# The first layer's MLP by two by two blocks with seven block products, its inner layer kept in DRAM

## The chip, the core and the metric

The kernel runs on one core of a Trainium2 chip. The metric is the device time of one execution in microseconds; the median of the runs shown is compared. The engines are TensorE (PE, with PEld its weight loads), VectorE (DVE), ScalarE (ACT), GpSimd (POOL) and SyncE (SP, which issues most DMAs).

## What is computed

Two layers over 512 latent and 256 context tokens of width 1024, 768 tokens in all. Each layer has three parallel token mixers and then the MLP that the change touches:

```python
def sq_relu_mlp(h, w1, w2):
    return jnp.square(jax.nn.relu(h @ w1)) @ w2

# per layer, D_FF = 4096
hx2 = rmsnorm(x, g_mlp[i]) * (1.0 + sc2x) + sh2x
x = x + g2x * sq_relu_mlp(hx2, w_ff1[i], w_ff2[i])
# in all layers but the last the same for the context tokens
```

All is float32. The last layer needs the latent tokens alone, so the first layer works on 768 tokens and the second on 512.

## The kernel before

Activations lie transposed: a page is a tile of 128 channels by up to 768 tokens, and `pg` hands out 46 such pages. A float32 product is made of three matmuls of a shorter type: each operand is split into a high part, a rounded copy, and a low part, the difference, and `mm_T` (L427 on) issues high by high, high by low and low by high for each of the 8 slices of 128 of the inner dimension. 768 tokens go as segments of 512 and 256 columns.

Weights come as pages of 128 by 1024 numbers (eight 128 by 128 blocks, one output tile) through `Stream`: `load` issues the DMA on SP into one of `NRAW` raw buffers, `split` makes the high part (POOL at L246, or ACT at L244) and `flush` the low part (DVE at L257). `ahead` keeps this one page ahead, with one more load.

The MLP of a layer runs in four chunks c of 1024 inner channels. `ff1(m, sg)` makes one inner tile: 24 matmuls for each segment, relu on ACT (L1661), the square on POOL (L1662), the split on ACT and DVE (L391, L392). Then eight output tiles of the chunk's second product are added to x, scaled by a gate, on DVE (L1686). In the first layer the second product of c = 3 is made in two token groups (`two`, L1700), so that the next layer's norm can begin.

The norm ahead of the MLP runs in two token groups of 384 (`even`). `norm_tail` is a generator: `sum` and `rstd` make the scale per token, `spread` broadcasts it by matmul (L507), and `finish` then scales (L524), shifts (L531) and splits the eight tiles. The second group's tail runs in the background while PE works on the first group's columns of the first five inner tiles (LEAD = 5).

Background generators are advanced by `tick`, once for every 6 matmuls in the MLP; `bg.rate` and `mbg.rate` say how many steps a tick gives. `mods_gen(1)` makes the next layer's modulation in the background at rate 0.3: pairs of multiplications on DVE with accumulation (L371 over 768, L373 over 256 elements, both inputs in SBUF), fed by SP loads into four `ld` buffers. It has 98 steps, of which 66 carry such a pair: 36 of the first 48, and 30 of the last 50.

Each engine takes its instructions in the order in which the program writes them.

Of the kernel before, what the change touches and what calls it, by code (L numbers as in the profile page):

```python
# [21 lines left out]
LAT = 512  # L22
# [15 lines left out]
NRAW = 2  # L38
# [10 lines left out]
def _page_shape(key):  # L49
    kind = key[0]  # L50
    if kind in ("in", "o", "ff1", "ff2", "lru"):
        return 8, 128
    if kind == "tok":
        return key[5], key[3]
    if kind == "qb":
        return key[4], 384
    if kind == "kvb":
        return 2, 512
    if kind == "br":
        return 8, 128  # L60
    raise KeyError(kind)
# [82 lines left out]
def kernel(ctx: ExitStack, tc: tile.TileContext, A: dict, order: list, record: bool, tap=None):  # L144
# [38 lines left out]
    ALT = ("AD", "PD")  # L183
    WOR = 1
# [35 lines left out]
    class Stream:  # L220
# [5 lines left out]
        def load(self, j):  # L226
            while self.nraw <= j and self.nraw < len(order):
                k = order[self.nraw]
                a, b = _page_shape(k)
                t = wp.tile([128, 1024], F32, tag="wr", bufs=NRAW, name=nm("wr"))[:, :a * b]  # L230
                nc.sync.dma_start(t, A["wst"][woff[k]:woff[k] + 128 * a * b].rearrange("(p n) -> p n", p=128))
                self.raw[self.nraw] = t
                self.nraw += 1

        def split(self, j):
            while self.nsp <= j and self.nsp < len(order):
                self.load(self.nsp)
# [22 lines left out]
        def get(self, key):  # L260
            if record:
                order.append(key)
            assert order[self.nget] == key, (order[self.nget], key)
            self.split(self.nget)
            if self.nsp == self.nget + 1:
                self.flush()
            self.nget += 1
            return self.hl.pop(self.nget - 1)

# [43 lines left out]
    rope = cst.tile([128, 2, 4, 32], F32, name="rope")  # L313
# [6 lines left out]
    x_d = drp.tile([8, 128, LAT], F32, name="x_d")  # L320

# [238 lines left out]
    def proj_tok(keys_, hi, lo, toks, N):  # L560
# [24 lines left out]
        return ds_  # L585

# [336 lines left out]
    nc.sync.dma_start(rope, A["rope"])  # L923
# [24 lines left out]
    for i in range(depth):  # L948
# [17 lines left out]
        def small_gen():  # L966
# [3 lines left out]
                                     in1=vc[:, V_MKN:V_MKN + 1], op0=ALU.mult, op1=ALU.mult)  # L970
            for w in range(2):
# [652 lines left out]
        nrm2 = Norm(i, x, V_GMLP, 32, 24, grp)  # L1624
        nf = None
        for g, parts in enumerate(grp):
# [3 lines left out]
            for m in range(8):  # L1630
# [4 lines left out]
                nrm2.stat(m, g, SQ0 if g else None)  # L1635
            if g == 0:
                nf = bg.add(norm_tail(nrm2, 0, *(TL0, TL4)[i]), front=True)
# [6 lines left out]
        mark(f"L{i} mlp")  # L1644
        W.defer = DF[5]
# [176 lines left out]
```

## Time and profile before

| | us |
|---|---|
| median of 3 runs | 2652.65 (2652.08 to 2658.22) |
| the profiled execution | 2651.59 |
| its span, first to last instruction | 2649.8 |
| PE busy | 2486.3 (94%) |
| DVE, POOL, ACT busy | 1614.6, 895.8, 797.6 |
| first layer's MLP, first product to the last chunk's second product | 981.7 to 1470.9 |

The span is what the engines' records cover; the time of the execution lies 1.8 us above it. Rows of a window give the busy time of each engine in it with the count of instructions, the granted clock of PE (1.00 is 2.4 GHz), and the DMA rate. A row of the timeline gives the start, the length, the engine and line, and in brackets the idle time before it and what ended it. Matmul lengths overlap in the pipeline; the spacing of starts is their rate.

### The profile page before, as it was taken

What the parts mean: (1) busy time and instruction counts of PE and PEld (TensorE: products, weight loads), DVE (VectorE), ACT (ScalarE), POOL (GpSimd) and SP (SyncE); (2) the same over time, 40 slices, a digit from 0 to 9 for tenths busy, and PEclk for the clock granted to TensorE, in tenths of its full rate; (3) what the DMA queues carried; (4) which work ended last, traced back from release to release, by engine and by line L of the source; (5) the groups of instructions that cost most, each with busy time, mean ns of one, the idle gap of its engine ahead of it and who ended that gap; (6) DMA issues with size and microseconds to landing.
All of it is one profiled execution on the core that took longest, in us unless ns stands there. A gap on an engine that the chain in (4) does not pass through costs nothing.

```text
span 2649.8 us, 38124 instructions
## 1 busy us (share of the span) xinstructions
PE 2486.3 (94%) x14406; PEld 2194.4 (83%) x14406; DVE 1614.6 (61%) x3303; ACT 797.6 (30%) x1945; POOL 895.8 (34%) x822
## 2 busy tenths in 40 slices
PE   6978999999899998999999989899998898899999
PEld 6868889898788898888888877789887787788887
DVE  7878665775785575655452467565655876643343
ACT  2261241425682122010101125433325741201100
POOL 5232122243342355222222352222253534633222
PEclk6999999999899999999999999999999999899999
DMA  6234322332014433334431322322221045333332
GB/s 222 80 108 157 122 91 88 114 115 83 7 57 167 144 112 110 127 110 145 153 139 61 120 96 80 111 98 78 86 95 55 1 154 166 120 118 95 96 96 96
DMA packets 93255, 282.97 MB, mean 107 GB/s; under 512 B 11152, under 2 KB 11920, under 8 KB 93072
## 3 DMA queue, kind: packets, MB, share of 16 engines
q1 hardware_dynamic: 84240, 257.46, 28.9%
q10 hardware_dynamic: 6912, 15.73, 1.6%
q0 software_dynamic: 1920, 7.34, 0.7%
q8 instruction: 114, 1.87, 0.3%
q14 instruction: 69, 0.57, 0.1%
HBM read 255.33 MB, written 25.17 MB: 106 GB/s over the span
## 4 chain that ended last, share of the span: by engine, by line
PE 65%; DVE 19%; ACT 6%; issue 5%; POOL 4%; DMA 1%; SPq 0%; ACTq 0%; DVEq 0%; POOLq 0%
PE f L438 32%; PE gt L1111 7%; PE S L745 4%; PE pt L576 4%; PE pt L577 4%; PE pt L578 4%; DVE wl L257 3%; PE pv L794 3%; PE T L771 2%; PE br L438 2%; PE wo L438 2%; DVE u L1019 1%; DVE junk L371 1%; ACT junk_a L1408 1%; POOL xn L531 1%
## 5 line engine op out<-in xcount | busy, mean ns | idle before, releaser
L246 POOL TENSOR_SCALAR wh<-wr 128x1024 fp32r<-128x1024 f32 (+2 forms) x297 | 335.9, 1133 | 635.8 <-DMA wr<-wst 244.0
L257 DVE TENSOR_TENSOR wl<-wr,wh 128x1024 fp32r<-128x1024 f32 (+1 forms) x286 | 391.2, 1369 | 151.3 <-POOL wh L246 113.3
L438 PE MATMUL f<-h,wh 128*128 128x512 f32 (+2 forms) x808 | 282.8, 350 | 9.8 <-ACT rl L1661 9.1
L438 PE MATMUL f<-l,wh 128*128 128x512 f32 (+2 forms) x808 | 282.3, 349 | 3.2 <-DVE l L392 3.2
L438 PE MATMUL f<-h,wl 128*128 128x512 f32 (+2 forms) x808 | 280.3, 347 | 0.7 <-DVE wl L257 0.7
L438 PE MATMUL f<-uh,wh 128*128 128x512 f32 (+1 forms) x768 | 273.8, 356 | 5.2 <-DVE x L1700 3.5
L438 PE MATMUL f<-ul,wh 128*128 128x512 f32 (+1 forms) x768 | 273.3, 356 | 0.0
L438 PE MATMUL f<-uh,wl 128*128 128x512 f32 (+1 forms) x768 | 272.1, 354 | 0.0
L631 POOL TENSOR_SCALAR P<-P,rl 128x768 f32<-128x768 f32 (+2 forms) x160 | 136.9, 856 | 384.3 <-DVE rl L630 274.8
L1111 PE MATMUL gt<-h,wh 128*128 128x512 f32 (+1 forms) x576 | 220.0, 382 | 6.8 <-POOL wh L246 5.9
L392 DVE TENSOR_TENSOR ul<-rl,uh 128x768 fp32r<-128x768 f32 (+3 forms) x74 | 66.6, 899 | 255.0 <-ACT uh L391 255.0
L577 PE MATMUL pt<-wl,h 128*128 128x256 f32 (+2 forms) x720 | 211.4, 294 | 10.0 <-DVE wl L257 10.0
L1661 ACT ACTIVATE rl<-f 128x768 f32<-128x768 f32 (+3 forms) x74 | 46.7, 632 | 573.7 <-PE f L438 573.7
L576 PE MATMUL pt<-wh,h 128*128 128x256 f32 (+2 forms) x720 | 214.1, 297 | 5.4 <-POOL wh L246 3.3
L1111 PE MATMUL gt<-h,wl 128*128 128x512 f32 (+1 forms) x576 | 207.7, 361 | 8.8 <-DVE wl L257 8.8
L578 PE MATMUL pt<-wh,l 128*128 128x256 f32 (+2 forms) x720 | 211.0, 293 | 0.0
L1111 PE MATMUL gt<-l,wh 128*128 128x512 f32 (+1 forms) x576 | 208.1, 361 | 0.0
L1662 POOL TENSOR_TENSOR rl<-rl 128x768 f32<-128x768 f32 (+3 forms) x74 | 85.8, 1159 | 315.2 <-ACT rl L1661 315.2
L402 DVE TENSOR_TENSOR ptl<-T,pth 128x384 fp32r<-128x384 f32 (+2 forms) x288 | 132.2, 490 | 97.8 <-ACT pth L396 96.3
L438 PEld LDWEIGHTS f<-h,wh 128*128 128x128 f32 x808 | 155.0, 192 | 29.7 <-issue 5.6
L438 PEld LDWEIGHTS f<-l,wh 128*128 128x128 f32 x808 | 154.8, 192 | 21.5 <-DVE l L392 4.4
L438 PEld LDWEIGHTS f<-h,wl 128*128 128x128 f32 x808 | 154.3, 191 | 18.7 <-DVE wl L257 1.1
(279 smaller groups left out, 6235.3 us busy)
## 6 DMA issues: line engine op xcount, KB each, us to landing
wr<-wst SPq DMA_DIRECT2D x298, 512.0 KB, 3.5
mod<-wmod SPq DMA_DIRECT2D x108, 384.0 KB, 4.3
bias<-bias SPq DMA_DIRECT2D x32, 320.0 KB, 3.6
th_d<-th ACTq DMA_DIRECT2D x24, 384.0 KB, 2.4
thr<-th_d SPq DMA_DIRECT2D x24, 384.0 KB, 3.5
x<-x SPq DMA_DIRECT2D x16, 384.0 KB, 4.9
th_d<-th ACTq DMA_DIRECT2D x24, 256.0 KB, 2.0
thr<-th_d SPq DMA_DIRECT2D x24, 256.0 KB, 3.8
```

The source lines that it names most:

```text
L246: pool.tensor_scalar(hi, t, 1.0, 0.0, op0=ALU.mult, op1=ALU.add)
L257: eng.tensor_tensor(out=lo, in0=t, in1=hi, op=ALU.subtract)
L402: dve.tensor_tensor(out=lo, in0=ps, in1=hi, op=ALU.subtract)
L438: pe.matmul(ps[:, c:c + b - a], wt[:, k, :], mv[k][:, a:b], start=k == 0 and wt is wh and mv is hi, stop=k == kts - 1 and wt is wl)
L576: pe.matmul(o, hi[kk][:, c], wh[:, k, :], start=kk == 0, stop=False)
L577: pe.matmul(o, hi[kk][:, c], wl[:, k, :], start=False, stop=False)
L578: pe.matmul(o, lo[kk][:, c], wh[:, k, :], start=False, stop=kk == total - 1)
L631: pool.tensor_scalar(self.P[:, :w], self.P[:, :w], rl, 1.0, op0=ALU.mult, op1=ALU.mult)
L745: pe.matmul(S[:, c:c + ww], a[r0:r1, qc], b[r0:r1, k0:k0 + ww], start=i_ == 0, stop=i_ == 2)
L794: pe.matmul(o[:, a:b], v_block(V, t, h), mv, start=i_ == 0, stop=i_ == len(ops) - 1, skip_group_check=True)
L1111: pe.matmul(ps[:, :b - a], wt[:, k, :], mv[k][:, a:b], start=k == 0 and wt is wh and mv is hi, stop=k == KT - 1 and wt is wl)
L1662: pool.tensor_tensor(out=t[:, a:b], in0=t[:, a:b], in1=t[:, a:b], op=ALU.mult)
```

## The change

In the first layer (`BLK = (True, False)`) the two products of the MLP are computed by blocks. Output channels are taken in pairs of tiles (m and m + 4), the inner dimension of a product in two halves of 512, and tokens in two halves of 384 columns, which gives 2 by 2 by 2 blocks. A Strassen-Winograd scheme forms a pair's four output blocks from seven block products (12 matmuls of 384 columns each) in place of eight. There are 16 pairs for the first product and 12 for chunks 0 to 2 of the second; chunk 3 stays as it was.

- **Weights**: `BlockWeights` holds two raw pages of a pair; POOL makes four sums of 128 by 512 from them, in place where it can, and ACT and DVE split each of the seven operands. Splits are five products ahead. `NRAW` becomes 3 for the whole kernel, and the `rope` table moves from its own buffer into a loaded page in each layer.
- **Activations**: `block_tail` replaces `norm_tail`; for the second token group it also forms sums of blocks and splits seven operands for each of 4 slices.
- **Inner layer**: all 16 pairs of the first product run first. The squared blocks and their sums are stored to DRAM (`u_d`) by ACT's queue, loaded again by SP six products ahead of use, and split by ACT and POOL three products ahead.
- **Order**: `seq` lists (pair, product). The first five pairs have products 1 and 2 made ahead on the first token group. Ticks come twice for each product, and `mods_gen(1)` starts at product 39.

```diff
-NRAW = 2
+NRAW = 3
+    BLK = (True, False)
+    BLEAD = (5, 5)
+    BAHEAD = 5
+    BLOAD, BSPLIT = 6, 3
+    TB0 = 6, 8, 4, "DPDPDPDP"
+    TB1 = 5, 4, 1, "DPDPDPDP"
+    u_d = [drp.tile([16, 3, 128, TOK], F32, name=f"u_d{i}") for i in range(depth)]
...
+    BLOCKS = {1: ("w11", "11"), 2: ("w12", "21"), 3: ("s4", "22"), 4: ("w22", "4"), 5: ("s1", "1"), 6: ("s2", "2"), 7: ("s3", "3")}
...
+        def sums(self, j):
+            if j < len(self.seq) and self.seq[j][1] == 6:
+                p = self.seq[j][0]
+                w11, w21, w22 = self.half(p, 0, 0), self.half(p, 1, 0), self.half(p, 1, 1)
+                pool.tensor_tensor(out=w11, in0=w11, in1=w21, op=ALU.subtract)
+                s2 = self.f[p, "s2"] = pg("s2")[:, :512]
+                pool.tensor_tensor(out=s2, in0=w22, in1=w11, op=ALU.subtract)
+                pool.tensor_tensor(out=w21, in0=w21, in1=w22, op=ALU.add)
+        def split(self, j):
...
+            if q == 6:
+                s4 = self.f[p, "s4"] = pg("s4")[:, :512]
+                pool.tensor_tensor(out=s4, in0=self.half(p, 0, 1), in1=src, op=ALU.subtract)
+            t = self.t[p, name] = wp.tile([128, 1024], F32R, tag="wh", bufs=8, name=nm(name))
+            split_block(t, 512, src)
...
+    def split_block(t, n, src, eng=dve):
+        act.activation(t[:, :n], src, AF.Copy)
+        eng.tensor_tensor(out=t[:, n:2 * n], in0=src, in1=t[:, :n], op=ALU.subtract)
...
+                for eng, o, p, q in ((pool, b3, b22, b12), (dve, b12, b12, b11), (dve, b2, b22, b12), (pool, b21, b21, b2)):
+                    eng.tensor_tensor(out=o, in0=p, in1=q, op=ALU.subtract)
+                yield
+                for j, (name, src, eng) in enumerate((("2", b2, dve), ("1", b12, dve), ("3", b3, pool), ("4", b21, pool), ("22", b22, dve))):
+                    O[name][kk] = pg("h" + name, F32R)
+                    split_block(O[name][kk], n, src, eng)
...
+        for k in range(KT) if g == 0 else (0, 4, 1, 5, 2, 6, 3, 7):
...
+            for p in range(BLEAD[i]):
+                seq += [(p, 1), (p - 1, 2)] if p else [(p, 1)]
+            seq.append((BLEAD[i] - 1, 2))
+            for p in pairs:
+                for q in (6, 5, 7, 3, 4) if p < BLEAD[i] else (1, 3, 6, 5, 7, 2, 4):
...
+            dmul = lambda t: pool.tensor_tensor(out=t, in0=t, in1=t, op=ALU.mult)
...
+            def add(out, ps, t):
+                dve.tensor_tensor(out=out, in0=ps[:, :n], in1=t, op=ALU.add)
...
+                        act.dma_start(u_d[i][p, slot][:, :2 * n], S[p][k][:, :2 * n])
...
+                    def sums():
+                        Z = st["Z"] = pg("bz")
+                        for o, a, b in ((Z[:, h1], Y[:, h1], Y[:, h0]), (Y[:, h0], Y[:, h0], X[:, h0]), (Z[:, h0], Y[:, h1], Y[:, h0])):
+                            pool.tensor_tensor(out=o, in0=a, in1=b, op=ALU.subtract)
+                    if last or p < 12:
+                        later(j + 1, sums)
+                    later(j + 4, lambda: store(p))
...
+            def xadd(m, h, src):
+                for s, a, b in grp[h]:
+                    dve.scalar_tensor_tensor(out=x[m][:, a:b], in0=src[:, a - h * n:b - h * n], scalar=mods[i][:, s, 40 + m:41 + m],
+                                             in1=x[m][:, a:b], op0=ALU.mult, op1=ALU.add)
...
+                if j == nlead:
+                    bg.finish(nf)
+                    bg.rate = 0.5
+                if not last and j == nlead + 5 * BLEAD[i] + 4:
+                    spread_c()
+                    mgen = mbg.add(mods_gen(i + 1))
+                    mbg.rate = 0.3
+                BW.ahead(j + BAHEAD)
...
+                for o, name in splits.get(j, ()):
+                    vs = uf.pop((o, name))
+                    if name == "4":
+                        for k in range(4):
+                            pool.tensor_tensor(out=vs[k], in0=vs[k], in1=vs[4 + k], op=ALU.subtract)
+                    for k in range(4):
+                        O[o][name][k] = pg("u" + name, F32R)
+                        split_block(O[o][name][k], n, vs[k], pool)
...
+                for k in range(4):
+                    for i_, (w0, b0) in enumerate(((0, 0), (0, n), (512, 0))):
+                        pe.matmul(ps, wt[:, w0 + 128 * k:w0 + 128 * k + 128], B[k][:, b0:b0 + n],
+                                  start=fresh and k == 0 and i_ == 0, stop=k == 3 and i_ == 2, skip_group_check=True)
+                    if k % 2:
+                        tick()
```

Between the last of `seq` and chunk 3, eight stored tiles are loaded whole, split on ACT and in turn on DVE and POOL (`plain_load`, `plain_split`), and the weight stream `W` starts again.

## Rows read from the trace of the kernel before

**Rows 1.** The page: busy time by engine, and the chain that ended last.

```profile
PE 2486.3 (94%) x14406; PEld 2194.4 (83%) x14406; DVE 1614.6 (61%) x3303; ACT 797.6 (30%) x1945; POOL 895.8 (34%) x822
...
PE 65%; DVE 19%; ACT 6%; issue 5%; POOL 4%; DMA 1%; SPq 0%; ACTq 0%; DVEq 0%; POOLq 0%
```

**Rows 2.** Windows: length, then busy (count) of PE, PEld, DVE, ACT, POOL; clock, DMA.

```profile
0.00:100.00 100.00, 78.10 (x402) 69.75 (x403) 74.39 (x174) 26.42 (x35) 48.00 (x33) 0.78 0.51 184
981.60:1024.00 42.40, 32.22 (x169) 29.78 (x169) 26.52 (x44) 11.97 (x25) 31.48 (x34) 0.96 0.19 69
1076.30:1470.70 394.40, 394.40 (x2256) 346.10 (x2255) 189.48 (x394) 38.16 (x46) 85.49 (x69) 1.00 0.34 121
981.60:1470.70 489.10, 478.92 (x2735) 424.03 (x2735) 245.83 (x486) 61.76 (x90) 137.15 (x119) 1.00 0.34 119
```

**Rows 3.** Timeline of PE: starts twelve matmuls apart, 512 and 256 mixed, then 384.

```profile
1080.27 0.40 PE L438 MATMUL f<-uh,wh 128*128 128x512 f32 x1
...
1082.37 0.40 PE L438 MATMUL f<-uh,wh 128*128 128x512 f32 x1
```

**Rows 4.** The same of the 384-column matmuls of the lead.

```profile
990.50 0.33 PE L438 MATMUL f<-h,wl 128*128 128x384 f32 x1
...
992.58 0.33 PE L438 MATMUL f<-h,wl 128*128 128x384 f32 x1
```

**Rows 5.** Timeline of PE around the lead's end: rows with idle time before them.

```profile
996.10 0.91 PE L507 MATMUL R<-sq,ones_f 128*128 128x384 f32 x2 [1.63 <-POOL sq L497]
...
1014.34 0.66 PE L438 MATMUL f<-h,wh 128*128 128x384 f32 x1 [5.34 <-ACT rl L1661]
...
1022.50 0.44 PE L438 MATMUL f<-h,wl 128*128 128x384 f32 x1 [0.74 <-DVE wl L257]
```

**Rows 6.** Timeline of DVE and POOL, four instructions that meet.

```profile
962.41 1.23 DVE L257 TENSOR_TENSOR wl<-wr,wh 128x1024 fp32r<-128x1024 f32 x1 [1.60 <-ACT wh L244]
962.49 2.03 POOL L524 TENSOR_TENSOR xn<-x,sq 128x384 f32<-128x384 f32 x1
963.55 1.37 DVE L392 TENSOR_TENSOR l<-xn,h 128x384 fp32r<-128x384 f32 x1
964.63 1.23 POOL L531 TENSOR_SCALAR xn<-xn,G,mods 128x384 f32<-128x384 f32 x1
```

**Rows 7.** Single lines around the first layer's MLP: count, shortest, median, longest (ns).

```profile
L392 DVE TENSOR_TENSOR l<-xn,h x16: 544/546/1385, 963.6 to 1020.1; 128x384 fp32r<-128x384 f32 x16
...
L371 DVE SCALAR_TENSOR_TENSOR junk<-mod,sB x58: 947/951/1803, 1080.6 to 1379.7; 128x768 bf16<-128x768 f32 x58
...
L373 DVE SCALAR_TENSOR_TENSOR junk<-mod,sB x59: 424/425/1140, 1079.5 to 1380.7; 128x256 bf16<-128x256 f32 x59
...
L1633 DVE SCALAR_TENSOR_TENSOR x<-wo,g1h,x x24: 336/469/618, 916.9 to 987.2; 128x384 f32<-128x384 f32 x8, 128x128 f32<-128x128 f32 x8, 128x256 f32<-128x256 f32 x8
...
L477 POOL TENSOR_TENSOR sq<-sq,sq x6: 1009/1016/1024, 926.1 to 983.1; 128x384 f32<-128x384 f32 x6
...
L1662 POOL TENSOR_TENSOR rl<-rl x7: 822/829/1207, 988.7 to 1028.7; 128x384 f32<-128x384 f32 x7
...
L531 POOL TENSOR_SCALAR xn<-xn,G,mods x16: 449/558/2132, 998.8 to 1017.0; 128x128 f32<-128x128 f32 x8, 128x256 f32<-128x256 f32 x8
```

**Rows 8.** Groups by line and shape: count, then busy us and mean ns.

```profile
L257 POOL TENSOR_TENSOR wl<-wr,wh 128x384 fp32r<-128x384 f32 x4 | 4.1, 1028 | 0.3
...
L477 POOL TENSOR_TENSOR sq<-sq,sq 128x512 f32<-128x512 f32 x3 | 3.9, 1308 | 0.1
...
L392 DVE TENSOR_TENSOR ul<-rl,uh 128x768 fp32r<-128x768 f32 x26 | 24.9, 958 | 126.7 <-ACT uh L391 126.7
...
L391 ACT ACTIVATE uh<-rl 128x384 fp32r<-128x384 f32 x10 | 5.3, 525 | 21.4 <-POOL rl L1662 21.4
```

**Rows 9.** DMA: rate by slices of 10 us from 1076, and the weight loads.

```profile
GB/s 136 133 131 101 143 127 52 172 93 54 172 143 54 219 124 183 168 96 216 156 110 153 155 133 131 171 110 247 132 185 52 52 54 52 55 64 95 53 55 52
...
wr<-wst SPq DMA_DIRECT2D x298, 512.0 KB, 3.5
```

More of the change, by code (lines that the diff above doesn't have):

```diff
@@ L268, in get, with bar @@
             return self.hl.pop(self.nget - 1)
+        def bar(self):
+            self.flush()
+            if record:
+                order.append(BAR)
+            assert order[self.nget] == BAR and self.nsp == self.nraw == self.nget
+            self.nget = self.nsp = self.nraw = self.nget + 1
         def ahead(self):
@@ L970, in small_gen @@
                                      in1=vc[:, V_MKN:V_MKN + 1], op0=ALU.mult, op1=ALU.mult)
+            rope = ld("rope")[:, :256].rearrange("p (a b n) -> p a b n", a=2, n=32)
+            nc.sync.dma_start(rope, A["rope"])
+            yield
             for w in range(2):
@@ L1624, with bkeys @@
         nrm2 = Norm(i, x, V_GMLP, 32, 24, grp)
+        if BLK[i]:
+            n = nq // 2
+            pairs = list(range(16 + 4 * (4 if last else 3)))
+            oset = lambda p: 0 if p < 16 else 1 + (p - 16) // 4
+            O = [{name: [None] * 4 for name in U_AT} for _ in range(5)]
+            hf = {}
+            def bkeys(p):
+                if p < 16:
+                    m = 8 * (p // 4) + p % 4
+                    return ("ff1", i, m), ("ff1", i, m + 4)
+                c, m = divmod(p - 16, 4)
+                return ("ff2", i, c, m), ("ff2", i, c, m + 4)
+            seq, prev = [], None
+            for p in range(BLEAD[i]):
[3 more added lines that the diff above has]
+                for q in (6, 5, 7, 3, 4) if p < BLEAD[i] else (1, 3, 6, 5, 7, 2, 4):
+                    if q != 3:
+                        seq.append((p, q))
+                    elif prev is not None:
+                        seq.append((prev, 3))
+                prev = p
+            seq.append((prev, 3))
         nf = None
@@ L1635 @@
                 nrm2.stat(m, g, SQ0 if g else None)
+                if BLK[i] and g and m >= 6:
+                    if m == 6:
+                        BW = BlockWeights(seq, [bkeys(p) for p in range(len(pairs))])
+                        BW.load()
+                    else:
+                        W.bar()
+                        BW.ahead(1)
             if g == 0:
-                nf = bg.add(norm_tail(nrm2, 0, *(TL0, TL4)[i]), front=True)
+                nf = bg.add(block_tail(nrm2, 0, O[0], hf, n, *TB0) if BLK[i] else norm_tail(nrm2, 0, *(TL0, TL4)[i]), front=True)
         bg.finish(nf)
```

261 lines of the change are left out of this document (259 added, 2 removed).

## The prediction

> **What bounds the kernel now.** I read the page first, then windows over the first layer's MLP, then single lines. TensorE is busy 94% of the span and the chain is PE for 65% [rows 1]. In the MLP the bound is plainer: from 1076.3 to 1470.7 PE is busy all 394.4 us at full clock, while DVE has 189.5, POOL 85.5 and ACT 38.2 us of work [rows 2]. Every matmul removed there is worth its spacing, as long as the other engines keep up. So two things must be priced: the matmuls, and the work on DVE and POOL that is added for them.
>
> **Spacing.** Twelve matmuls, half of 512 and half of 256 columns, take 2.10 us [rows 3]; twelve of 384 columns take 2.08 us [rows 4]. The same columns cost the same, 0.175 and 0.1733 us a matmul.
>
> **What DVE and POOL do to each other.** Four instructions meet [rows 6]. DVE starts a weight subtraction at 962.41 and ends at 963.64. POOL's product starts at 962.49, 1.02 us long when alone (as at L477) [rows 7], takes 2.03 and ends at 964.51, 0.88 after DVE's end. DVE's next subtraction, 0.55 us when alone [rows 7], starts at 963.55, takes 1.37 and ends at 964.92, 0.41 after POOL's end. POOL's next one again waits for that. They take turns, and only about 0.13 us of each POOL and 0.14 us of each DVE instruction lies under the other's. It holds for DVE instructions with both inputs in SBUF: those with an input in PSUM never exceed 0.618 us in 24 (L1633) [rows 7]. Before the change this costs little: 189.5 + 85.5 us, not all of it on this path, in 394.4 us [rows 2].
>
> The Trainium skill, page "SBUF — State Buffer", section "Who interferes with whom", speaks against this change: a VectorE instruction with two SBUF inputs and a GpSimd instruction that reads SBUF exclude each other, and the later one waits until the first has finished. Read strictly, whole instructions would add up; the rows agree on the turns but let 0.13 to 0.14 us overlap, and the measurement decides. What the strict rule gives is the rival "whole instructions" below.
>
> **Prices on this shared path** (duration alone less the overlap). POOL with two inputs, 384 columns: 1.016 [rows 7], the very split operation 1.028 [rows 8], so 0.88; 512 columns 1.308 [rows 8], so 1.18; a square in place 0.829 [rows 7], so 0.70; a shift of a tile in two pieces 0.449 + 0.558 [rows 7], so 0.75. DVE split of 384: 0.41. Of 512 no row stands; between 0.546 for 384 [rows 7] and 0.958 for 768 [rows 8] I take 0.68 by the line, so 0.54. A modulation pair 0.951 + 0.425 [rows 7], so 1.10. An addition into x from SBUF 0.47 for 384 columns, 0.53 for 128 and 256 (0.618, 0.336, 0.469 [rows 7], less the overlap).
>
> **The change, part by part.**
>
> *Matmuls.* Before, 28 pairs x 96: 2448 at 0.175 and the lead's 240 at 0.1733, 470.0 us. After, 28 x 84 = 2352 at 0.1733, 407.7 us. Removed: 62.3 us. A pair now takes PE 14.56 us, a second pass of a lead pair (five products) 10.4.
>
> *A later pair of the first product.* POOL: four weight sums 4.72, four squares 2.80, three sums of blocks 2.64. DVE: seven splits 3.78. Path 13.9 us, under PE's 14.56: pair 5 runs at PE's speed. From pair 6 modulation runs too: 14 ticks x 0.3 = 4.2 steps, 0.75 of them with a pair, 3.45 us: path 17.4 us, six pairs 104.3. Pairs 12 to 15 form no sums of blocks: 14.75, together 59.0.
>
> *The lead pairs' second pass.* POOL 4.72 + three squares 2.10 + 2.64, DVE five splits 2.70: 12.2 us against PE's 10.4; five 60.8.
>
> *A pair of the second product.* POOL 4.72; DVE splits 3.78, modulation 4.2 x 0.6 x 1.10 = 2.76, additions into x from SBUF 1.53: 12.8 us, under PE. But for every group of four pairs the stored blocks come back: 28 splits and 4 differences, all on POOL, 28.2 us, in one pair's time. Four pairs have 51.2 + 28.2 = 79.4 us on the path and 58.2 on PE: 19.8 a pair, 238 for twelve.
>
> *The hand-over after the lead.* The five first passes end on PE near 1009: 981.7 + 20.8 + some 6 us of waits for the norm, which stay. The tail can begin only when the scale is spread, 997 [rows 5]. What it and its neighbours then put on the path: POOL four scales 3.5, eight shifts 6.0, eight block differences 7.0, eight splits 7.0, weight sums 3.5, squares 2.5; DVE four scales, eight differences and twelve splits 9.8, weights 3.8; 43.1 in all, less 2.6 that stand behind the first product's last operand. So that product ends near 1038.5 in place of 1010.5: PE waits 28 us. Before it waited 6.8 there, in four places of which the longest and the last stand in [rows 5].
>
> *Given back:* weights are split five products ahead, about 8 us of path work that need not be done in time. *Chunk 3's start:* POOL four subtractions of 768 (twice a 384, 1.8 each), DVE four and the stream's own splits, some 16 us of path in the last six products, 12.5 us of PE: 3 us.
>
> *Sum.* 20.8 + 28 + 60.8 + 14.6 + 104.3 + 59.0 + 238 - 8 + 3 = 520.5 us, against 470.0 + 6.8 = 476.8: 43.7 longer.
>
> *Edits with small prices.* The third raw buffer lets every page's load start a page earlier in the whole kernel: DMA is 1% of the chain [rows 1], so the gain lies between 0 and 26 us; 5 taken, since the MLP, its largest user, has no such wait. ACT: some nineteen copies of about 0.53 [rows 8] for a pair, 10 of 14.6 us, hidden. Its 48 stores stand behind POOL's last sum, and weight copies queue behind them; that delay is POOL's, already counted, and the data are read at least four pairs later. On SP the 32 loads of a group wait for pages, and modulation and weight loads queue behind them: 6.3 MB at the best slice's 247 GB/s [rows 9] are 25 us, under a 40 us stretch of path; 0 taken, up to 9 a group if POOL were faster. The rope load hides under the layer's first projections; uncovered, about the 3.5 of a weight load [rows 9], twice. The clock: in 981.6:1024 PE had 32.2 of 42.4 us and 0.96; in the first 100 us, 78% busy, 0.78 [rows 2]. If the lead's wait brought 0.78 over such a stretch, 7 us; 0 taken.
>
> **Forecast.** 2651.59 + 43.7 - 5 = 2690 us. The profiled execution lies 1.06 us under the median, which changes nothing here.
>
> **Rivals.**
>
> *POOL alone* (faster). If DVE always gives way without being late itself, POOL's own durations decide: PE waits 21 at the hand-over, the lead pairs take 10.8 each, plain pairs follow PE, and a returning group needs 32.5 on POOL plus 8.9 of weight sums in 25 us of PE plus some 8 of running ahead, 8.5 late three times. 20.8 + 21 + 54.1 + 160.2 + 174.7 + 25.5 + 3 = 459.3, 17.5 less: with the buffer's 5, 2629. For it: the blocks are listed ahead, and queues run ahead of PE. Against: DVE itself was held up [rows 6].
>
> *DMA behind it* (no change). The same, with 9 us of loads in each group: 2656.
>
> *PE alone* (faster). All is hidden: 407.7 + 6.8 against 476.8, 62.3 less, 2584 with the buffer. Against: POOL's 32.5 us in a pair's time.
>
> *Whole instructions* (slower still). By full durations: hand-over 38, lead pairs 14.2, pair 5 16.4, pairs 6 to 11 20.7, 12 to 15 17.7, second product 23.9: 20.8 + 38 + 71 + 16.4 + 124.2 + 70.8 + 286.8 - 8 + 3 = 623, 146 longer, 2792. It would also stand in for a clock that falls in the waits.
>
> *Eight products after all:* 2688 matmuls would stay; the diff's `seq` has seven to a pair, so only the count of rows can refute it; no chance given.
>
> **How the numbers follow.** Forecast 0.50, by itself 2660 to 2735; whole instructions or part of the way there 0.14; POOL alone 0.20; PE alone 0.06; DMA behind it, or gain and loss that cancel, 0.10. Slower by over 0.3% (8 us, about what a measurement of this kernel can tell from no change): 0.50 + 0.14 = 0.64. Faster: 0.20 + 0.06 and 0.01 of the cancelling case, 0.27. Within: 0.09. The range leaves out PE alone, the better edge of POOL alone and the worse half of whole instructions: 2622 to 2755.
>
> **What would show it.** 2352 matmuls of 384 columns in the blocks, 0.173 us apart where PE does not wait. PE idle about 28 us after the ten first products, ended by a `split_block` line on DVE or ACT behind POOL. Three stretches in the second product, one where each group returns, each with POOL busy nearly throughout and PE waiting 15 to 25 us for a split of stored blocks. POOL's two-input rows of 384 with a mean well over 1.02 and DVE's splits of 512 over 0.68. PE busy in pairs 6 to 11 at about 84%. Wrong it is if POOL and DVE together exceed the length of a stretch and PE still does not wait: then the turns cost less than [rows 6] say.

## The result and the profile after

The changed kernel takes 2851.53 us (median of four, 2850.63 to 2853.6) against 2652.36 us before in the same session: a ratio of 1.0749, 95% interval 1.073 to 1.0767. The forecast was 2690 with a range up to 2755. The direction was right, the loss five times too small: +199 us where +38 were expected.

The page of after, busy time and chain, which answer to [rows 1]:

```profile
PE 2505.5 (88%) x14070; PEld 2233.4 (78%) x14070; DVE 1816.0 (64%) x3533; ACT 959.5 (34%) x2308; POOL 1167.5 (41%) x1055
...
PE 54%; DVE 19%; POOL 10%; issue 8%; ACT 6%; DMA 3%; SPq 0%; ACTq 0%; POOLq 0%; DVEq 0%
```

PE's share of the chain falls from 65 to 54%, though fewer matmuls run. POOL's rises from 4 to 10, "issue" from 5 to 8 and DMA from 1 to 3.

**Where it went.** By PE's first and last block matmul the block stretch runs from 987.5 to 1653.2; the same work took 981.7 to 1470.9 before. That is 665.8 against 489.2 us, 176.6 longer. The rest lies outside it: 7.5 in the output projection ahead of it, 2.6 at chunk 3, 12.4 in the second layer up to its MLP and 3.5 in that, less 1.7 at the beginning: 200.9 in all, and the spans differ by 200.8.

Windows of after by stage: length, then busy (count) of PE, PEld, DVE, ACT, POOL; clock, DMA. In order: first and second pass of the lead pairs, pair 5, pairs 6 to 11, pairs 12 to 15, the three chunks of the second product, and all of them:

```profile
987.50:1027.20 39.70, 25.82 (x135) 24.28 (x136) 20.81 (x35) 13.31 (x28) 21.03 (x20) 0.89 0.22 76
1027.20:1136.40 109.20, 62.88 (x302) 58.39 (x301) 46.56 (x65) 27.85 (x54) 71.70 (x69) 0.78 0.20 73
1136.40:1163.60 27.20, 20.95 (x117) 20.44 (x117) 10.70 (x13) 10.06 (x20) 17.38 (x16) 0.87 0.41 155
1163.60:1289.40 125.80, 102.43 (x506) 98.71 (x505) 89.73 (x147) 40.35 (x82) 77.95 (x65) 0.89 0.40 148
1289.40:1368.70 79.30, 65.95 (x338) 62.26 (x337) 54.45 (x95) 28.18 (x59) 47.33 (x39) 0.94 0.45 161
1368.70:1464.60 95.90, 71.04 (x339) 64.90 (x338) 66.33 (x116) 38.34 (x81) 64.10 (x53) 0.84 0.49 178
1464.60:1563.20 98.60, 70.22 (x338) 63.36 (x337) 68.87 (x110) 34.74 (x71) 65.01 (x51) 0.88 0.46 163
1563.20:1653.20 90.00, 69.50 (x337) 64.88 (x338) 77.93 (x118) 29.81 (x56) 59.43 (x45) 0.85 0.55 192
...
987.50:1653.20 665.70, 488.81 (x2399) 457.23 (x2400) 435.36 (x693) 222.64 (x450) 423.92 (x352) 0.86 0.40 146
```

Against [rows 2] DVE's work in the MLP grew from 245.8 to 435.4 us and POOL's from 137.2 to 423.9. But no engine is full here: POOL is busy 64% of the stretch, DVE 65%, ACT 33%. And the clock, 1.00 before, is 0.78 to 0.94.

**Floor, clock, waits.** The distance from each of the 2352 block matmuls to the next sorts itself: 0.173 us (the floor of [rows 4]), some 0.32 us, or a wait of over 0.4. What the second class has above 0.1733 us stands under "clock", what the third has above it under "waits":

| stage | length | floor | clock | waits | waits forecast |
|---|---|---|---|---|---|
| lead pairs, both passes | 148.9 | 72.8 | 7.4 | 68.3 | 36.8 |
| pair 5 | 27.2 | 14.6 | 0.5 | 12.1 | 0 |
| pairs 6 to 11 | 125.8 | 87.4 | 12.2 | 25.8 | 16.9 |
| pairs 12 to 15 | 79.3 | 58.2 | 5.2 | 15.5 | 0.8 |
| second product | 284.5 | 174.7 | 23.0 | 85.9 | 63.3 - 8 |
| all | 665.8 | 407.7 | 48.3 | 207.6 | 109.8 |

The forecast column is the prediction's stage sums less the floor. The floor came out as forecast. The waits are nearly twice as long, 98 us more. Of the 48 us under "clock" some 41 are matmuls at the lower clock, which had been taken as 0; the other 7 are the first distance behind a wait, 0.28 us at full clock.

**How a wait is made.** A timeline of after, one pair of the first product (rows of other engines left out):

```profile
1208.24 0.55 DVE L1851 TENSOR_TENSOR by<-fc,by 128x384 f32<-128x384 f32 x1
1208.82 0.52 ACT L1847 ACTIVATE by<-by 128x384 f32<-128x384 f32 x1 [3.52 <-DVE by L1851]
...
1209.42 0.83 POOL L1842 TENSOR_TENSOR by<-by 128x384 f32<-128x384 f32 x1 [4.95 <-ACT by L1847]
...
1210.33 1.34 POOL L1901 TENSOR_TENSOR bz<-by 128x384 f32<-128x384 f32 x1
...
1211.75 1.34 POOL L1901 TENSOR_TENSOR by<-by,bx 128x384 f32<-128x384 f32 x1
...
1213.17 1.61 POOL L1901 TENSOR_TENSOR bz<-by 128x384 f32<-128x384 f32 x1
...
1214.74 1.44 POOL L648 TENSOR_TENSOR wr<-wr,wr 128x512 f32<-128x512 f32 x1
1216.26 1.26 POOL L650 TENSOR_TENSOR s<-wr,wr 128x512 f32<-128x512 f32 x1
...
1217.55 0.63 ACT L681 ACTIVATE s<-s 128x512 fp32r<-128x512 f32 x1 [6.79 <-POOL s L650]
1218.09 0.47 ACT L1884 ACTIVATE by<-fb 128x384 f32<-128x384 f32 x1
...
1218.61 6.00 PE L2011 MATMUL fb<-h,w 128*128 128x384 f32 x24 [3.88 <-ACT by L1884]
```

DVE adds, ACT applies relu, POOL squares, forms three sums of blocks and the next pair's weight sums; ACT then copies such a sum. That copy is needed five products later, yet it stands in ACT's queue ahead of the evacuation L1884, for whose bank PE waits. The round trip is 10.4 us, 1208.24 to 1218.61. POOL has work in it from 1209.42 almost to the end, but POOL, too, had waited 4.95 us for ACT. Each engine waits in turn.

The waits of after over pair 6 to the end of the blocks, us in total, times, longest:

```profile
ACT s L681 <- POOL s L650: 98.5, 18, 13.5
DVE s L682 <- ACT s L681: 90.0, 38, 14.3
ACT by L1847 <- DVE by L1851: 60.1, 21, 4.2
ACT u L681 <- POOL uf L1987: 52.9, 12, 18.2
POOL wr L648 <- DVE w L682: 50.2, 9, 18.4
POOL by L1842 <- ACT by L1847: 50.1, 13, 4.9
PE fb L2011 <- ACT by L1925: 41.9, 8, 9.5
...
PE fb L2011 <- ACT by L1884: 25.6, 10, 3.9
```

Read as a ring: ACT for POOL, POOL for DVE and ACT, DVE for ACT, ACT for DVE. PE's own longest entries name ACT's evacuations L1925 and L1884, which have nothing to do with POOL except their place in the queue.

**The clock.** Windows of after across that wait:

```profile
1208.00:1212.00 4.00, 4.00 (x24) 3.79 (x24) 2.82 (x5) 1.95 (x4) 2.42 (x3) 1.00 0.88 330
1212.00:1216.00 4.00, 2.73 (x16) 2.41 (x14) 3.04 (x5) 0.00 (x0) 3.92 (x3) 1.00 0.00 0
1216.00:1220.00 4.00, 1.39 (x6) 1.39 (x7) 1.79 (x2) 1.01 (x2) 3.92 (x4) 0.93 0.41 160
1220.00:1224.00 4.00, 4.00 (x17) 4.00 (x17) 2.85 (x6) 1.05 (x2) 1.25 (x2) 0.64 0.36 139
```

PE runs 24 matmuls in 4 us at 1.00, waits 3.88 us, and is then busy all 4 us for only 17, at a granted clock of 0.64, part of it at the lower of its two levels (1.2 GHz). This follows the wait in pair after pair: 351 of the 2352 matmuls lie 0.26 to 0.40 us behind the one before, 0.320 in the median. 286 of them fall where the granted clock is at that lower level; the other 65 stand right behind a wait, at full clock. Such a stretch counts as busy PE: of the 102.43 us in pairs 6 to 11 (fourth of the stage windows above) only 87.4 are matmuls at full rate.

### The profile page after: what moved, and what is told of

Its sections match the earlier page's. It is cut to its first block, busy times and chain, and to the rows that moved or that the text cites. A ratio compares the mean times of both kernels' runs of the same rounds, so it can differ in the third digit from the quotient of the medians.

```text
span 2850.6 us, 38722 instructions
## 1 busy us (share of the span) xinstructions
PE 2505.5 (88%) x14070; PEld 2233.4 (78%) x14070; DVE 1816.0 (64%) x3533; ACT 959.5 (34%) x2308; POOL 1167.5 (41%) x1055
## 4 chain that ended last, share of the span: by engine, by line
PE 54%; DVE 19%; POOL 10%; issue 8%; ACT 6%; DMA 3%; SPq 0%; ACTq 0%; POOLq 0%; DVEq 0%
PE f L457 13%; PE gt L1259 8%; PE S L891 4%; PE pt L595 4%; PE pt L596 4%; PE pt L597 4%; PE br L457 3%; PE pv L940 3%; DVE wl L268 2%; PE T L917 2%; PE lu L457 2%; DVE junk L390 2%; PE fb L2011 2%; PE wo L457 2%; POOL u L682 1%
## 5 line engine op out<-in xcount | busy, mean ns | idle before, releaser
L390 DVE SCALAR_TENSOR_TENSOR junk<-mod,sB 128x768 bf16<-128x768 f32 x132 | 156.9, 1189 | 22.4 <-DMA mod<-wmod 21.7
L415 ACT ACTIVATE pth<-T 128x384 fp32r<-128x384 f32 (+2 forms) x288 | 115.3, 440 | 152.5 <-PE T L917 148.0
L596 PEld LDWEIGHTS pt<-wl,h 128*128 128x128 f32 x720 | 139.6, 194 | 11.8 <-DVE wl L268 11.7
L457 PE MATMUL f<-uh,wh 128*128 128x512 f32 (+1 forms) x384 | 143.8, 375 | 4.8 <-DVE x L2039 4.8
L457 PE MATMUL f<-uh,wl 128*128 128x512 f32 (+1 forms) x384 | 143.2, 373 | 0.0
L457 PE MATMUL f<-ul,wh 128*128 128x512 f32 (+1 forms) x384 | 143.2, 373 | 0.0
L595 PEld LDWEIGHTS pt<-wh,h 128*128 128x128 f32 x720 | 139.3, 193 | 4.9 <-POOL wh L257 1.8
L597 PEld LDWEIGHTS pt<-wh,l 128*128 128x128 f32 x720 | 139.5, 194 | 0.0
L1259 PEld LDWEIGHTS gt<-h,wl 128*128 128x128 f32 x576 | 111.3, 193 | 34.8 <-DVE wl L268 18.0
L1259 PEld LDWEIGHTS gt<-h,wh 128*128 128x128 f32 x576 | 111.8, 194 | 29.7 <-POOL wh L257 6.1
L2011 PE MATMUL fb<-h,w 128*128 128x384 f32 x444 | 97.7, 382 | 42.5 <-ACT by L1884 25.6
```

The lines of the kernel that those rows point to most:

```text
L390: dve.scalar_tensor_tensor(out=junk, in0=t, scalar=1.0, in1=sB[s], op0=ALU.mult, op1=ALU.mult, accum_out=acc[:, s, j, 0:1])
L415: act.activation(hi, ps, AF.Copy)
L457: pe.matmul(ps[:, c:c + b - a], wt[:, k, :], mv[k][:, a:b], start=k == 0 and wt is wh and mv is hi, stop=k == kts - 1 and wt is wl)
L595: pe.matmul(o, hi[kk][:, c], wh[:, k, :], start=kk == 0, stop=False)
L596: pe.matmul(o, hi[kk][:, c], wl[:, k, :], start=False, stop=False)
L597: pe.matmul(o, lo[kk][:, c], wh[:, k, :], start=False, stop=kk == total - 1)
```

## The experiments

Times are medians of four executions or more; the runs with free weights, with free sums, with short modulation pairs, without POOL's pair work and with two constant writes have a single one each. Four executions of one kernel lie up to 8 us apart, so an effect of under 5 us says little.

**The third raw buffer alone, and the rope table alone.** `BLK` off leaves the prior MLP with three raw buffers and the moved table; with `NRAW = 2` besides, the table alone.

```diff
-    BLK = (True, False)
+    BLK = (False, False)
```

> The block scheme switched off in both layers, so that only the third raw weight buffer and the moved rope load remain of the change. The prediction took 5 us off for them. Up to the output projection of the first layer the changed kernel ran 1.7 us ahead of the one before, but its second layer took 16 us more. If the buffer or the rope load caused that, this kernel takes 2660 to 2668 us; if the second layer's loss comes from what the blocks leave behind, 2645 to 2652.

> Block scheme off and two raw weight buffers as before: only the rope load's new place is left of the change. With three buffers the same kernel was 0.39% slower than the one before. If the third buffer costs that, this one takes 2650 to 2656; if the rope load does, about 2664.

Measured 2664.44 (ratio 1.0039, 1.0024 to 1.0054) and 2653.5 (1.0005, 0.9996 to 1.0015). The table costs nothing; the third buffer costs some 10 us where 5 were counted as a gain. From the second layer's first product to its output projection 681.8 us stand against 673.5 before. There PE's wait for a weight split has grown (waits of PE in the second layer, of before and of the run with the buffer):

```profile
PE gt L1111 <- DVE wl L257: 2.6, 2, 1.6
```

```profile
PE gt L1259 <- DVE wl L268: 7.5, 2, 7.3
```

Why an earlier load should delay that split was not followed further.

**Nothing waits for the weight sums; nothing waits for any sum.** POOL makes the same three weight sums into a page that no one reads, and the splits read raw halves; then the stored blocks' differences go the same way. The operands are not the scheme's.

```diff
-                pool.tensor_tensor(out=w11, in0=w11, in1=w21, op=ALU.subtract)
+                pool.tensor_tensor(out=s2, in0=w11, in1=w21, op=ALU.subtract)
...
-pool.tensor_tensor(out=vs[k], in0=vs[k], in1=vs[4 + k], op=ALU.subtract)
+pool.tensor_tensor(out=vs[4 + k], in0=vs[k], in1=vs[4 + k], op=ALU.subtract)
```

> POOL makes the same four weight sums of 128 by 512 for each pair, but three of them into a scratch page, and the splits of those operands read the raw weights: the block products use wrong weights, the work on every engine stays. Theory of order: ACT and DVE carry the evacuations of the products just made behind weight copies that wait for POOL's sums; without that wait PE's waits for evacuations shrink, 60 to 110 us less, 2740 to 2790. Theory of the shared path: POOL and DVE still take the same turns, so no more than 10 us less, 2840 or above.

> As the kernel with free weights, and the four differences of stored blocks go to the page that is not split, so that ACT's copies do not wait for POOL there either (the products use wrong operands there). ACT waited 53 us for these differences. Theory of order: 20 to 40 us less than with free weights alone, near 2725, and the block stretch, 665.8 us in the changed kernel, comes near the 533 of the prediction's sum of turns. Theory of the shared path alone: no change.

2827.54 and 2818.84: 24 and 33 us back, where the theory of order had expected 60 to 110 and 20 to 40 more, and that of the shared path 10 at most. Both missed, and the second step, 9 us between two single executions, is hardly clear of noise. The edit takes more away than ACT's waits: as the sums no longer overwrite the raw halves, POOL's own wait for DVE's splits (L648, 50.2 us in the list above) goes too. In pairs 6 to 11 ACT's wait for POOL's sums, 38.8 us in after, was gone, but its relu's wait for DVE's add grew, here in after and with free sums:

```profile
ACT by L1847 <- DVE by L1851: 31.0, 12, 4.2
```

```profile
ACT by L1847 <- DVE by L1851: 49.6, 12, 7.4
```

The wait had changed hands, half of it.

**Sums of blocks behind the next pair's weight sums**, order alone:

```diff
-                        later(j + 1, sums)
+                        after_w.setdefault(j + 2, []).append(sums)
```

> Only an order is changed: POOL's three sums of squared blocks, some 3.7 us for a pair, stand behind the weight sums of the next pair instead of ahead of them; the work and the result are the same. Theory of order: the weight copies on ACT are released some 3 us earlier in each of the twelve pairs, and with them the evacuations: 20 to 40 us less, 2810 to 2830. Theory of the shared path: no change, within 5 us of 2851.

2846.59 (1.0721, 1.0703 to 1.0738): 5 us. The theory of order missed here; which of POOL's sums comes first matters little.

**Short modulation pairs.** DVE's multiplications for layer 1's modulation take 32 columns; layer 2 gets wrong modulations.

```diff
-                dve.scalar_tensor_tensor(out=junk, in0=t, scalar=1.0, in1=sB[s], op0=ALU.mult, op1=ALU.mult,
+                dve.scalar_tensor_tensor(out=junk[:, :nb], in0=t[:, :nb], scalar=1.0, in1=sB[s][:, :nb], op0=ALU.mult, op1=ALU.mult,
```

> The modulation pairs of the second layer work on 32 columns in place of 768 and 256 (the second layer then runs on wrong modulations); their number, steps and loads stay. The prediction charged the shared path 3.45 us of them for each of ten pairs of the first product and 2.76 for each of twelve of the second, 67.6 us. Theory of the shared path (turns set the time): 60 to 75 us less, about 2783. Theory of order (the engines wait on one another in program order, not for lack of time): under 30 us less, 2820 or above.

2793.78: 58 us back, near the 68 charged and well above the 30 that the theory of order allowed. This run shortens DVE's own queue and the turns at once, so it does not tell the two apart.

**POOL's pair work left out**: no weight sums, no sums of blocks, no low parts of stored blocks, squares on 32 columns.

> POOL's part of the block pairs is left out, apart from squares of 32 columns: no weight sums, no sums of squared blocks, no differences and low parts of stored blocks (PE reads the high part twice there). Loads, stores, ACT, DVE and PE keep their work. Both theories expect most of the loss back: with PE's pace in all pairs and only the hand-over of the tail left, the block stretch takes about 455 of the 666 us, 2640 in all. If more than 2700 remains, DVE and ACT alone, without POOL, hold PE up, and POOL is not the cause.

2688.53: 163 back, and still 36 above before; some 2640 had been expected. So most of the loss needs POOL's work, and a part does not. The lead's passes take 113.9 us against a floor of 72.8: the hand-over costs 41 by itself.

**Constant writes in place of POOL's sums**: two, then three whole ones, then three narrower ones that add up to about the sum's lone length. POOL reads nothing from SBUF there; only in the norm tail and at chunk 3 it still does, in 34 us of work. A write waits for whatever holds the place it writes, but no longer for an operand that was only read.

```diff
+    def fill(t):
+        m = t.shape[-1]
+        c = {384: 294, 512: 408}[m]
+        for a in (0, m - c, 0):
+            pool.memset(t[:, a:a + c], 0.01)
-                pool.tensor_tensor(out=w11, in0=w11, in1=w21, op=ALU.subtract)
+                fill(w11)
```

> Each two-input POOL instruction of the block pairs becomes two writes of a constant over the same columns: POOL stays busy for a similar time and every wait stays, but it reads no SBUF (the block operands are wrong). If such writes do not take turns with DVE, DVE's splits of 512 columns fall back to about 0.68 us. Theory of the shared path: POOL's own durations are then all that counts, and the time is that of the rival POOL alone, near 2660 to 2690. Theory of order: POOL's bursts still hold ACT's copies and with them the evacuations, so no more than 60 us less, 2790 or above. It depends on how long the writes take: POOL's busy time in the stretch has to stay near the 380 us of the changed kernel.

> As the run with two constant writes in place of each two-input POOL instruction of the block pairs, but with three: POOL reads nothing from SBUF there and keeps every wait, and its own work is now longer than the sums were when alone (3 x 0.418 = 1.25 us for 384 columns against 1.02, 3 x 0.526 = 1.58 for 512 against 1.31). If the turns on the shared path made the loss, DVE's splits of 512 stay at 0.69 us and most of the 122 us stays given back: 2740 to 2785. If it was the length of POOL's own queue that made it, POOL's longer work brings the time to after's or beyond: 2840 to 2900.

> As the runs with two and three constant writes in place of each two-input POOL instruction of the block pairs, but three narrower writes (294 of 384 columns, 408 of 512), sized from the rows 0.418 and 0.526 so that together they take about what the sum took alone: 1.02 and 1.31 us. POOL then reads nothing, holds DVE up nowhere, keeps its waits and has the length it would have without any turns. If the turns with DVE are the loss and POOL's own length is not, it stays with the two-write run (2729): 2725 to 2750, and the rest up to 2851.5 is what the turns cost. If POOL's own length in a chain of hand-overs is the loss, it lies on the line between two writes (POOL busy 320 us in the stretch, 2729) and three (465 us, 2836): at about 390 us 2780 (2765 to 2800), and the turns cost the 70 that are left.

2729.18, 2835.98 (1.0688, 1.0672 to 1.0704) and 2789.7 (1.0511, 1.0495 to 1.0527). Windows over the block stretch of the three runs, in this order, columns as above:

```profile
987.10:1529.80 542.70, 449.78 (x2399) 433.49 (x2400) 315.01 (x689) 223.29 (x450) 305.34 (x667) 0.92 0.50 177
```

```profile
988.00:1632.00 644.00, 483.33 (x2399) 445.59 (x2400) 316.09 (x689) 222.91 (x450) 448.85 (x983) 0.87 0.42 150
```

```profile
991.80:1589.00 597.20, 467.17 (x2399) 440.48 (x2400) 315.64 (x689) 223.17 (x450) 374.29 (x983) 0.89 0.45 161
```

DVE's 315 to 316 us are the same in all three, so the writes do not hold it up; only POOL's length differs: 305, 374, 449 us give stretches of 543, 597, 644. Each microsecond on POOL costs 0.6 to 0.8 us, although POOL is idle 30 to 44% of the time. Near its lone length (597.2) next to nothing shares a path, and the stretch is 189 us over the floor. What the turns add is 665.7 - 597.2 = 68.5 us of the stretch; in time, 2851.5 - 2789.7 = 62. That is their least, since the squares, too, became three writes, each of 0.345 us (a group of the last run):

```profile
L683 POOL MEMSET by<- 128x294 f32 x84 | 29.0, 345 | 46.7 <-ACT by L1856 43.5
```

Three of them are 1.04 us, and a square alone takes 0.83 [rows 7]: 13 us too much for 64 squares, at the price above an estimated 8 to 11 us of the stretch.

The first of the three runs by itself looks like proof of the turns (122 us back). It is not: two writes are also 20% shorter than the sum (0.84 for 1.02, 1.05 for 1.31), and the third run showed what that is worth. The second, 16 us under after, looks like proof against them, because its POOL has more than its lone work.

That DVE is held up by turns, on the other hand, is plain from the splits of 512 columns, here in after and in the last run (groups by shape: count, busy us, mean ns, idle before):

```profile
L682 DVE TENSOR_TENSOR w<-wr,w 128x512 fp32r<-128x512 f32 x65 | 52.3, 815 | 15.1 <-ACT w L681 14.0 <-DMA mod<-wmod 1.1
L682 DVE TENSOR_TENSOR s<-s,s 128x512 fp32r<-128x512 f32 x43 | 49.4, 1148 | 68.0 <-ACT s L681 67.6
...
L682 POOL TENSOR_TENSOR u<-uf,u 128x384 fp32r<-128x384 f32 x84 | 104.7, 1283 | 0.1
```

```profile
L689 DVE TENSOR_TENSOR w<-wr,w 128x512 fp32r<-128x512 f32 x65 | 44.2, 687 | 20.0 <-ACT w L687 18.8 <-DMA mod<-wmod 1.1
...
L689 DVE TENSOR_TENSOR s<-s,s 128x512 fp32r<-128x512 f32 x43 | 29.7, 690 | 96.6 <-ACT s L687 55.0 <-POOL u L683 41.5
```

815 and 1148 ns fall to 687 and 690; the estimate of 0.68 was right.

**Squares on ACT.**

```diff
-            dmul = lambda t: pool.tensor_tensor(out=t, in0=t, in1=t, op=ALU.mult)
+            dmul = lambda t: act.activation(t, t, AF.Square)
```

> The squares of the inner blocks go from POOL (both inputs in SBUF) to ACT's square function; nothing else changes. Turns on the shared path: four squares a pair of 0.70 to 0.83 us leave it, three for a lead pair, so pairs 6 to 11 fall from 21.0 to about 18, pairs 12 to 15 from 19.8 to about 17, pair 5 by 3, the lead pairs' second pass by 10 to 12: together some 45 us, 2806 (2795 to 2820). ACT has 45.6 of 125.8 us of work in pairs 6 to 11 and takes four times about 0.5 more. Order of ACT's queue (the squares stand ahead of evacuations there): a gain of 15 at most, or a loss: 2836 to 2865.

2848.07 (1.0733, 1.0717 to 1.0749), 3 us, which is within the noise, where the theory of turns had expected 45. Pairs 6 to 11 of that run, columns as above:

```profile
1161.50:1287.00 125.50, 101.15 (x505) 97.00 (x505) 86.83 (x143) 50.73 (x102) 57.71 (x42) 0.90 0.40 148
```

POOL has 20 us less, ACT 10 more, the length is the same. The square has only moved to another engine of the same ring; a bound by the sum of DVE's and POOL's work is refuted here.

**Splits behind the evacuation**, order alone: POOL's sums stay, ACT's and DVE's splits are issued after the product's evacuation. Each copy then also has one product (2.1 us) more behind its sum.

```diff
-                BW.ahead(j + BAHEAD)
+                BW.sums(j + BAHEAD + 1)
...
                 (evac1 if p < 16 else evac2)(j, p, q)
+                BW.ahead(j + BAHEAD)
```

> Order alone, all work kept: POOL's weight sums and the differences of stored blocks stay where they are, but ACT's and DVE's splits of weights and of stored blocks stand behind the evacuation of the product, not ahead of it; so an evacuation no longer stands behind a copy that waits for POOL, and a copy has one product (2.1 us) more behind its sum. Order theory (an in-order queue passes POOL's lateness on to PE): ACT's wait for POOL's sums falls from 6.5 us a pair to about 4, some 2 us for each of 28 pairs, and the waits of 18 us for returned blocks shrink: 2795 to 2825. Throughput of the shared path: the same work, within 10 us of 2851: 2841 to 2856.

2813.99 (1.0602, 1.0586 to 1.0618): 37 us back with all work kept. Pairs 6 to 11 fall from 125.8 to 110.2 us. Two waits of that run from 1130 to 1620, which is the part of after's list and 20 us of pair 5:

```profile
ACT s L682 <- POOL s L651: 55.5, 16, 5.7
ACT u L682 <- POOL uf L1992: 51.8, 12, 16.2
```

98.5 has become 55.5 (51.2 from pair 6 on). What reaches PE is told by the waits of PE that end at one of ACT's evacuations: over all blocks they were 97 us in after, 25.6 of them at L1884, and are 64 here, none of them at that line. So 32 of the 37 us are found where the theory of order has them. The returned blocks' wait (52.9) stays, and chunks 0 to 2 with it: 280.0 against 284.5 us.

**Both of ACT's waits away**: the free sums and the short pairs in one.

> Two earlier edits in one: ACT's copies wait for none of POOL's weight sums and stored-block differences (these still run, into pages that nothing reads), and the layer-1 modulation pairs on DVE take 32 columns. Left out: the seven weight operands are not the scheme's, and layer 2 gets wrong modulations. Alone they gave 33 and 58 us. If ACT's waits for POOL and DVE's lateness are separate losses, they add: 2760 (2750 to 2770). If they are two ways into one loop (ACT waits for whichever of the two is later), taking away both gives more than the sum, as each alone only hands the wait to the other: 2720 to 2750. If one loss was counted twice, less: 2775 to 2795.

2766.83 (1.0421, 1.0404 to 1.0439): 85 back, 33 + 58 less 6. The two losses add; they are not one counted twice.

**Norm tail five steps earlier; the order edits joined; weights seven products ahead.**

```diff
-    TB1 = 5, 4, 1, "DPDPDPDP"
+    TB1 = 0, 4, 1, "DPDPDPDP"
...
-    BAHEAD = 5
+    BAHEAD = 7
```

> The second token group's norm tail begins five background steps earlier (its sum of squares stands some 8 us earlier in PE's order). My hand-over term took the scale as spread 15.3 us after the first product; it is spread 16.9 after it, and the start itself is 5.8 later. If the chain of scale, shift, differences and splits sets the hand-over from that start, the lead's two stretches (148.9 us together) fall by 6 to 9 us: 2843. If the hand-over is set by what stands ahead of the chain in POOL's and DVE's queues (weight sums and weight splits), by less than 3: 2849 to 2852.

> Three changes of order together, all work kept: splits behind the evacuation, POOL's sums of squared blocks behind the next pair's weight sums, the second norm tail five steps earlier. Alone they gave 37, 5 and 0 us. If each removes waits of its own: 2809 (2800 to 2815). If the second and third matter only once ACT no longer stands in front (the wait had only changed hands): 2780 to 2800. If they cancel the first's room: 2816 to 2830.

> As the joined order, with weights made ready seven products ahead in place of five: sums and copies both two products (4.2 us) earlier. If what is left of ACT's wait for POOL's sums (5.7 us at the longest) is lateness that two products can cover, 15 to 30 us below the joined order. If POOL comes to these sums late because of what stands ahead of them in its own queue for the same pair, the head start is no cover: within 8 us of the joined order.

2851.79 (1.0746, 1.073 to 1.0762), 2811.72 (1.0598, 1.0582 to 1.0614) and 2805.66 (1.0573, 1.0555 to 1.0591). The second is the sum of its parts, and the two products' head start of the third gives 6 us more, as was expected if POOL comes to its sums late by what stands ahead of them in its queue. In the first, the lead's passes fell from 148.9 to 145.5 us, but the median did not move; as a small term of the whole it is not settled. Squares on ACT, sums behind the weight sums and the earlier tail in one kernel gave 2843.85 (1.0712, 1.0694 to 1.073), 8 us back, where turns alone should have given some 50 and the order of ACT's queue 16 at most. The last is the best kernel found that does the change's work, still 151 us over before.

## Why the prediction was wrong

**Matmuls** (62.3 us fewer): right. 2352 run, at 0.173 us where PE is not held up.

**What DVE and POOL do to each other**: the mechanism was right, its place in the sum wrong. They take turns, and it costs 62 us or somewhat more. But the prediction let the shared path's total set each stage. With next to no shared path the stretch is 597.2 us, more than the whole forecast of 520.5. The overlap of 0.13 and 0.14 us read from four instructions mattered little beside that.

**"That delay is POOL's, already counted"**, of ACT's stores behind POOL's last sum and the weight copies behind them: the step that failed, and with it the stage sums, which made the waits 109.8 us where they measured 207.6. The copies were priced by ACT's load (10 of 14.6 us, "hidden") and by whether their data come in time, not by what stands behind them in ACT's queue: evacuations for which PE waits. The order edit gave 37 us by moving the splits alone, 32 of them in PE's waits for evacuations. It also voids "given back": splits five products ahead cover the weights, not the evacuations that queue behind them.

**The stage sums** took the busier of PE and the path. The rows show a ring: DVE's add, ACT's relu, POOL's square and sums, ACT's copy, ACT's evacuation, PE. Its round trip counts, 10.4 us in the pair shown, whoever is idle meanwhile. It fits this that pairs 12 to 15, whose path of 14.75 us hardly exceeded PE's 14.56, wait 15.5 us, and that POOL near its lone length costs 100 us more (597.2) than when its pair work is left out (497.0). How the rest of the waits divides among the links of the ring was not measured. The sign "PE busy in pairs 6 to 11 at about 84%" nearly holds (102.43 of 125.8 us, 81%), but by slow matmuls: at full rate it is 69%.

**The clock "0 taken"**, 7 at most: some 41 us. The row at hand, 0.96 around the lead's waits [rows 2], held the price. It is one fall of the clock, where PE goes on after its longest wait there, 5.34 us [rows 5] (windows of before):

```profile
1010.00:1014.00 4.00, 0.00 (x0) 0.00 (x0) 2.71 (x5) 1.23 (x3) 3.27 (x4) 0.98 0.37 131
1014.00:1018.00 4.00, 3.66 (x13) 3.69 (x14) 0.61 (x2) 0.20 (x1) 3.66 (x6) 0.59 0.00 0
```

0.04 of 42.4 us is 1.7 us for one such fall. After has 25 of them in the block stretch, six in pairs 6 to 11. What the prediction lacked was their number; that 25 x 1.7 = 42 comes so near is in part luck, as the falls differ in length.

**The hand-over**: forecast 28 us of wait and 8.8 in the second passes, measured 68.3 in both. (The terms of its 1038.5, 997 and 40.5, give 1037.5.) The form was right, as PE's two longest waits there end at a `split_block` copy and at an evacuation behind one (waits of PE in the lead and pair 5, then the timeline of after):

```profile
PE fb L2011 <- ACT h L681: 25.4, 3, 10.2
```

```profile
1004.36 0.91 PE L526 MATMUL R<-sq,ones_f 128*128 128x384 f32 x2 [1.54 <-POOL sq L516]
...
1020.75 0.52 ACT L681 ACTIVATE h<-hs 128x384 fp32r<-128x384 f32 x1 [8.22 <-DVE hs L708]
...
1022.64 0.47 ACT L1866 ACTIVATE bx<-fb 128x384 f32<-128x384 f32 x1
...
1023.16 1.33 PE L2011 MATMUL fb<-h,w 128*128 128x384 f32 x3 [9.56 <-ACT bx L1866]
```

The spreading begins at 1004.36, not at 996.10 [rows 5], 5.8 us of it because the MLP begins later. For the rest the rows show the same order of ACT's queue, with a copy of the tail that waits 8.22 us for DVE ahead of the evacuation.

**The returning groups**: as foretold, three stretches with POOL full; in 1480 to 1500 POOL is busy 19.92 us and PE 9.55. But PE's long waits there, 8.0, 8.4 and 9.5 us, do not end at a split of stored blocks, as the prediction's sign had it. They end at ACT's evacuation L1925, which stands behind copies that waited for POOL's first difference (L1987), here in the second group (timeline of after):

```profile
1489.74 0.52 ACT L681 ACTIVATE u<-uf 128x384 fp32r<-128x384 f32 x1 [18.24 <-POOL uf L1987]
...
1493.55 0.47 ACT L1925 ACTIVATE by<-fb 128x384 f32<-128x384 f32 x1
...
1494.07 6.17 PE L2011 MATMUL fb<-u,w 128*128 128x384 f32 x20 [8.44 <-ACT by L1925]
```

Waits that end at a split of stored blocks are 16.5 us in all, none over 0.9. The 63.3 us forecast for the second product's waits became 85.9.

**Pair 5** and **the buffer**: pair 5's 12.1 us of waits include 5.9 for `spread_c`'s broadcast, which had no price; the buffer was 15 us off, gain for loss.

**The rivals.** "PE alone" and "POOL alone" fall. "Whole instructions" came nearest with 2792, and its stage figures seem confirmed: 20.7 and 23.9 a pair against 125.8 / 6 = 21.0 and 284.5 / 12 = 23.7. They are not. Of the 21.0 us, 14.6 are matmuls, 2.0 clock and 4.3 waits, and with squares off POOL the figure does not move. A sum that meets the measured number is not yet its cause. The Trainium skill, page "SBUF — State Buffer", section "Who interferes with whom", says that a two-input DVE instruction contends with a GpSimd instruction that reads SBUF, not with one that only writes it. The trace agrees: beside constant writes DVE's splits take 687 to 690 ns, beside sums up to 1148.

**What is settled and what is open.** Of the 177 us in the stretch: 258 over the floor, of which 68.5 or somewhat more are turns, 100 or somewhat less POOL's own length (with the waits and the clock that follow from it) and 89 remain with POOL's pair work out, the hand-over's 41 among them (the other 48 were not taken apart); less the 81.5 by which before lay over that floor (489.2 - 407.7). These are parts in one order of removal; others give other shares, as the order's 37 and the modulation's 58 overlap with them. Open are the 12 us in the second layer, of which the buffer explains some 8 to 10, and the 7.5 us ahead of the MLP.

## What to carry to other kernels

When a change hands a value through three or four engines for each product, add up the round trip and ask, for every instruction that can wait, what stands behind it in its queue; busy shares of 64, 65 and 33% did not say that PE would lose 208 us. Issue what frees a PE bank ahead of what is prefetched: that order alone was worth 37 us here. Fewer matmuls pay only while PE stays fed, as in this kernel the matmuls behind the longer waits ran slower as well.

## What was not expected of the hardware

The clock: in a stretch with a wait of 2 to 10 us in most pairs, one matmul in eight (286 of 2352) ran at the lower clock, some 41 us in all, and the page counts it as busy PE. And POOL's constant writes, 0.418 us for 384 columns and 0.526 for 512, leave DVE's splits of 512 columns at 684 to 691 ns, whether two or three stand for a sum, which makes them a probe that tells a neighbour's length from a neighbour's reads.
